# The final norm of the last token tile: a half in two pieces, two engines for the scaling, two queues for the store

## The chip, the cores and the metric

The kernel runs on one core of a Trainium2 chip. The metric is the device time of one execution in microseconds; before the change it was 1151.39 us, the median of three runs (1151.34 to 1152.82). About 0.2% (2.3 us) is what a measurement of this kernel can tell from no change.

## The reference, cut to what matters

Two transformer layers over 512 tokens of width 1024, each a token mixer and a dense MLP, then one last RMSNorm. The change touches the last projection of the second MLP and that norm:

```python
def rms_norm(x, g):
    xf = x.astype(jnp.float32)
    y = xf * lax.rsqrt(jnp.mean(xf * xf, axis=-1, keepdims=True) + EPS)
    return (y * g.astype(jnp.float32)).astype(x.dtype)

def squared_relu_mlp(h, w_up, w_down):
    a = jax.nn.relu(h @ w_up)
    return (a * a) @ w_down

        x = x + squared_relu_mlp(h, mlp_w_up[i], mlp_w_down[i])
    return rms_norm(x, final_norm)
```

## The kernel before, in words

The 512 tokens are four tiles of 128 rows (`NT` = 4); the residual `xt[t]` of each stays in SBUF as 128x1024 fp32. Products are taken in split precision: each operand is held as a high and a low part, and `mm3` (lines 227 to 229) issues three matmuls for one product. The MLP runs over 8 blocks of 512 hidden columns. The down projections of the first seven blocks go through `down_quarters`; the last block goes through `down` (line 1232), which is what the change edits.

`down` walks the four token tiles, and in each tile the two halves of 512 output columns. One half is 4 x 3 matmuls of 512 columns into one PSUM bank (`ps`, taken from banks 6, 7, 2, 3 in turn), then an addition of that bank into `xt[t]` by VectorE (line 1244), then the call `after(t, c)`. In the second MLP `after` is `Final.follow`, and it calls `rms_half`.

`rms_half` (line 430) does the final norm of a tile. On each half ScalarE squares `x` into the output tile `fo` as a throwaway and leaves the sum of the squares in a column of `rs_s` (line 436; on the chip an ACTIVATE and a short read of the accumulator). After the second half VectorE adds the two sums and the epsilon (line 440, 128x1), GpSimd raises this to the power -0.5 (line 441, `rs_y`, 128x1), and VectorE writes `x * y * gain` in two pieces of 512 columns (line 444). Behind each piece SyncE issues a store of 256 KB (line 1266), which waits for that piece alone. `fo` has two buffers, so a tile's first square waits for the stores of the tile two before it.

A scheduler orders each engine's instructions when the kernel is built; each engine then runs its own list in order and waits on semaphores. Behind the last store SyncE waits for all stores to land, and a barrier of all engines ends the program.

Of the kernel before, what the change touches and what calls it, by code (L numbers as in the profile page):

```python
# [11 lines left out]
F32 = mybir.dt.float32  # L12
F32R = mybir.dt.float32r
I32 = mybir.dt.int32
AF = mybir.ActivationFunctionType
OP = mybir.AluOpType
PSUM = bass.MemoryType.PSUM

P = 128
D = 1024  # L20
S = 512
NT = S // P
KD = D // P
CHUNK = 64
EPS = 1e-6
# [179 lines left out]
def trunk(ctx: ExitStack, tc: tile.TileContext, x, positions, attn_norm, mlp_norm, a_w_in, a_w_out,  # L205
          b_w_in, b_q_norm, b_kv_norm, b_w_q_up, b_w_kv_up, b_w_out, mlp_w_up, mlp_w_down,
          final_norm, out):
    nc = tc.nc
# [9 lines left out]
    class Banks:  # L218
        def __init__(self, *ids):
            self.ids, self.n = ids, 0  # L220
# [5 lines left out]
    def mm3(ps, lh, ll, rh, rl, first, last):  # L226
        nc.tensor.matmul(ps, lh, rh, start=first, stop=False)  # L227
        nc.tensor.matmul(ps, lh, rl, start=False, stop=False)  # L228
        nc.tensor.matmul(ps, ll, rh, start=False, stop=last)  # L229
# [3 lines left out]
    neghalf = const.tile([P, 1], F32, name="neghalf")  # L233
# [56 lines left out]
    ht = ctx.enter_context(tc.tile_pool(name="ht", bufs=1, reuse_waits="tile"))  # L290
# [5 lines left out]
    def gain(pool, row, n, tag="gain"):  # L296
        g = pool.tile([P, n], F32, name="gain", tag=tag)
        nc.sync.dma_start(g, bass.AP(tensor=row.tensor, offset=row.offset, ap=[[0, P], [1, n]]))
        return g

    xt = [const.tile([P, D], F32, name=f"x{t}") for t in range(NT)]
# [123 lines left out]
            cs = slice(c, min(c + 512, n))  # L425
            nc.vector.scalar_tensor_tensor(dst[:, cs], src[:, cs], y, g[:, cs], op0=OP.mult, op1=OP.mult)

    half_sums = []

    def rms_half(dst, src, g, c, done=None):  # L430

        cs = slice(c * 512, (c + 1) * 512)
        if c == 0:
            half_sums.append(ht.tile([P, 2], F32, name="rs_s", tag="rs2", bufs=3))
        ss = half_sums[-1]
        nc.scalar.activation(dst[:, cs], src[:, cs], AF.Square, scale=D ** -0.5, accum_out=ss[:, c:c + 1])
        if c == 1:
            half_sums.pop()
            y = ht.tile([P, 1], F32, name="rs_y", tag="rs", bufs=8)
            nc.vector.tensor_scalar(y, ss[:, 0:1], ss[:, 1:2], EPS, op0=OP.add, op1=OP.add)  # L440
            nc.gpsimd.tensor_tensor(y, y, neghalf, op=OP.pow)
            for i in range(2):
                cs = slice(i * 512, (i + 1) * 512)
                nc.vector.scalar_tensor_tensor(dst[:, cs], src[:, cs], y, g[:, cs], op0=OP.mult, op1=OP.mult)
                if done is not None:
                    done(cs)

    def to_feature_major(src, nk, hi, lo, t, banks):

        for k0 in range(0, nk, 4):  # L450
            n = min(4, nk - k0)
            ps = banks("tps")
            for k in range(n):
                nc.tensor.transpose(ps[:, k * P:(k + 1) * P], src[:, (k0 + k) * P:(k0 + k + 1) * P], ident)  # L454
            pv = ps[:, :n * P].rearrange("p (k t) -> p k t", k=n)
            h = hi[:, k0:k0 + n, t * P:(t + 1) * P]
            l = lo[:, k0:k0 + n, t * P:(t + 1) * P]
            nc.scalar.copy(h, pv)  # L458
            nc.vector.tensor_sub(l, pv, h.bitcast(F32))

    class Norm:
# [30 lines left out]
            with tc.high_priority(60):  # L492
                to_feature_major(self.h.pop(t), KD, self.hi, self.lo, t, self.banks)

        def follow(self, t, c):

            if c == 0:
                return
            if self.lag == 2 and t >= 2:
                self.turn(t - 2)  # L500
            self.scale(t)
            if self.lag == 1 and t:
                self.turn(t - 1)
# [13 lines left out]
    def out_proj(oh, ol, banks, after=None, held=0):  # L517

        n = oh.shape[1]
        ws = W.take(n, held)  # L520
        for t in range(NT):
            for c in range(2):
                cs = slice(c * 512, (c + 1) * 512)
                ps = banks("wo_ps")
                for j in range(n):
                    wh, wl = ws[j]
                    mm3(ps, oh[:, j, t * P:(t + 1) * P], ol[:, j, t * P:(t + 1) * P], wh[:, 0, cs], wl[:, 0, cs],
                        j == 0, j == n - 1)
                    if j % 2 == 1 and j < n - 1:
                        yield  # L530
                nc.vector.tensor_add(xt[t][:, cs], ps, xt[t][:, cs])
                if after is not None:
                    after(t, c)
                yield


# [162 lines left out]
    def mixer_a():  # L699
        with ExitStack() as sa:  # L700
# [255 lines left out]
            for i in range(2):  # L956
                for _ in proj_tiles(Banks(*((0, 1, 6, 7), (2, 3, 4, 5))[i]), lambda t, ps: q_done(i, t, ps)):
# [4 lines left out]
                    if n > 32 and n % 4 == 0:  # L962
                        plan.step(-6 + (n - 36) // 4)
            run(selection)
            plan.filler(44, 0.7, lazy(lambda: out_proj(*O[0], Banks(7))))
            plan.filler(60, 0.4, lazy(lambda: out_proj(*O[1], Banks(7))))
            plan.run()
            nm = Norm(mlp_norm[0], lag=2)
            run(out_proj(*O[2], Banks(4, 5, 6, 7), nm.follow))
        return nm  # L970

# [175 lines left out]
    def mlp(i, nm, follower):  # L1147
        with ExitStack() as sm:
# [3 lines left out]
            up_b, dn_b = Banks(0, 1, 4, 5), Banks(6, 7, 2, 3)  # L1152
# [11 lines left out]
            def up(b):  # L1164
                u = mp.tile([P, 4, S], F32, name="u", tag="u", bufs=2)
                if b == 0:

                    ws = W.take(2) + W.take(2, 2)
                    pp = [up_b("up") for _ in range(4)]
                    for f in range(4):  # L1170
                        up_mm(pp[f], ws[f // 2 * 2:][:2], f % 2, 0, S // 2)
                        if f % 2:
                            nm.turn(NT - 2 + f // 2)
                    for f in range(4):
                        up_mm(pp[f], ws[f // 2 * 2:][:2], f % 2, S // 2, S)
                        square(pp[f], u, f)
                    return u
                for c in range(FB // 256):
                    ws = W.take(2)
                    for f in range(2):  # L1180
                        ps = up_b("up")
                        up_mm(ps, ws, f, 0, S)
                        square(ps, u, 2 * c + f)
                return u

            def part(v):

                lh = mp.tile([P, 2, S // 2], F32R, name="lh", tag="lh", bufs=8)
                ll = mp.tile([P, 2, S // 2], F32R, name="ll", tag="ll", bufs=8)
                nc.scalar.copy(lh, v)  # L1190
                nc.vector.tensor_sub(ll, v, lh.bitcast(F32))  # L1191
                return lh, ll

            def blocks(u):

                return [[u[:, 2 * k:2 * k + 2, i * 256:(i + 1) * 256] for k in range(2)] for i in range(2)]
# [32 lines left out]
                        last = nc.vector.tensor_add(x[:, cs], pp[t], x[:, cs])  # L1229
                return last  # L1230

            def down(u, after):
                ops = [[part(v) for v in row] for row in blocks(u)]
                ws = W.take(FB // P)
                for t in range(NT):
                    ts = slice(t % 2 * P, (t % 2 + 1) * P)
                    for c in range(2):
                        cs = slice(c * 512, (c + 1) * 512)
                        ps = dn_b("dn")
                        for k in range(4):  # L1240
                            wh, wl = ws[k]
                            lh, ll = ops[t // 2][k // 2]
                            mm3(ps, lh[:, k % 2, ts], ll[:, k % 2, ts], wh[:, 0, cs], wl[:, 0, cs], k == 0, k == 3)
                        nc.vector.tensor_add(xt[t][:, cs], ps, xt[t][:, cs])
                        after(t, c)

            prev = up(0)
            last = None
            for b in range(1, NB):
                with tc.issue_after(last.ins) if last is not None else ExitStack():  # L1250
                    ops = left(prev)
                prev = up(b)
                last = down_quarters(ops)
            nxt = follower()
            down(prev, nxt.follow)
        return nxt

    class Final:
        def __init__(self):
            self.g = gain(ht, final_norm, D)  # L1260

        def follow(self, t, c):
            if c == 0:
                self.o = ht.tile([P, D], F32, name="fo", tag="h", bufs=2)
            o = self.o
            rms_half(o, xt[t], self.g, c, lambda cs: nc.sync.dma_start(out[0, t * P:(t + 1) * P, cs], o[:, cs]))

    nm = mixer_a()
    nm = mlp(0, nm, lambda: Norm(attn_norm[1]))
    nm = mixer_b(nm)  # L1270
    mlp(1, nm, Final)


# [22 lines left out]
```

## Time and profile before

| what | value |
|---|---|
| median of the runs | 1151.39 us (1151.34 to 1152.82) |
| the profiled execution's own time | 1150.95 us |
| its span | 1149.2 us |
| PE busy | 1117.5 us, 97% of the span |
| VectorE, ScalarE, GpSimd busy | 66%, 54%, 58% |
| granted TensorE clock, mean | 0.993 of full speed |

Engines are named PE (TensorE matmul), PEld (its weight loads), DVE (VectorE), ACT (ScalarE), POOL (GpSimd) and SP (SyncE); SPq is SyncE's issuing of DMAs. A timeline row gives the start in us from the span's start, the length in us, engine, line, operation, names (output<-input) and shapes; in brackets stands how long the engine was idle before it and what ended the wait. A span lies inside the execution's own time; 1.75 us lie around it.

### The profile page before, as it was taken

Reading aid. Unit: us, or ns where it says so; the run is one execution under the profiler, and the core shown is the slowest. Engines: PE = TensorE matmul, PEld = TensorE weight load, DVE = VectorE, ACT = ScalarE, POOL = GpSimd, SP = SyncE. Lnnn points to the kernel's source line nnn. Section 1 sums busy time; section 2 is a strip of 40 time slices with the busy share of each in tenths; the row PEclk is TensorE's granted clock in tenths of the full one; section 3 lists DMA queues with packets and bytes.
Section 4 is the critical chain, followed back from the end, with each engine's and each line's share of the span. In section 5 each row is a group of like instructions: output and inputs, shape, how many; then the busy total and the mean of one; then the engine's idle time right before and its main releaser. Section 6 shows DMA issues by size and latency. Waiting matters only on the chain.

```text
span 1149.2 us, 16018 instructions
## 1 busy us (share of the span) xinstructions
PE 1117.5 (97%) x5725; PEld 949.2 (83%) x5725; DVE 754.8 (66%) x1399; ACT 619.7 (54%) x1143; POOL 670.0 (58%) x508
## 2 busy tenths in 40 slices
PE   8999899989999999999999999899999999999997
PEld 7788788869888888888889898787988888888886
DVE  6699798673566466466566788676556466556664
ACT  6574896534544554454445776563564454464452
POOL 5498533543657857856702643554557756865772
PEclk9999999989999999999999999999999999999999
DMA  6413100242224314413322200111424313412402
GB/s 200 123 55 110 38 1 1 76 150 87 75 72 147 106 58 130 133 58 103 86 62 79 76 23 34 56 56 56 167 63 138 128 49 117 147 61 87 147 10 83
DMA packets 65465, 99.04 MB, mean 86 GB/s; under 512 B 3173, under 2 KB 41833, under 8 KB 65386
## 3 DMA queue, kind: packets, MB, share of 16 engines
q1 hardware_dynamic: 65386, 98.03, 26.9%
q8 instruction: 45, 0.74, 0.3%
q14 instruction: 34, 0.28, 0.1%
HBM read 95.92 MB, written 2.10 MB: 85 GB/s over the span
## 4 chain that ended last, share of the span: by engine, by line
PE 90%; DVE 3%; ACT 3%; issue 2%; POOL 1%; DMA 1%; SPq 0%; DVEq 0%; POOLq 0%; ACTq 0%
PE dn L1226 23%; PE up L227 10%; PE up L229 10%; PE up L228 10%; PE s_ps L560 3%; PE o_ps L622 3%; PE pt_ps L579 2%; PE wo_ps L227 2%; PE wo_ps L228 2%; PE wo_ps L229 2%; PE pp L227 2%; PE pp L229 2%; PE pp L228 2%; PE tps L454 1%; PE dn L228 1%
## 5 line engine op out<-in xcount | busy, mean ns | idle before, releaser
L148 POOL TENSOR_TENSOR w_lo<-quad,w_hi 128x512 fp32r<-128x512 f32 x196 | 274.7, 1433 | 163.1 <-ACT w_hi L143 155.7
L150 POOL TENSOR_TENSOR w_lo<-w_raw,w_hi 128x1024 fp32r<-128x1024 f32 (+4 forms) x117 | 264.4, 2278 | 86.7 <-ACT w_hi L143 71.6
L1229 DVE TENSOR_TENSOR x<-dn,x 128x512 f32<-128x512 f32 x196 | 134.9, 690 | 139.5 <-PE dn L1226 139.4
L228 PE MATMUL up<-hT_lo,w_hi 128*128 128x512 f32 (+1 forms) x576 | 210.8, 367 | 0.0
L227 PE MATMUL up<-hT_hi,w_hi 128*128 128x512 f32 (+1 forms) x576 | 210.3, 368 | 0.0
L229 PE MATMUL up<-hT_hi,w_lo 128*128 128x512 f32 (+1 forms) x576 | 208.8, 367 | 0.0
L143 ACT CAST w_hi<-w_raw 128x1024 fp32r<-128x1024 f32 (+6 forms) x112 | 111.7, 1006 | 141.1 <-PE dn L1226 62.2
L143 ACT CAST w_hi<-quad 128x1024 fp32r<-128x1024 f32 x98 | 101.2, 1050 | 100.0 <-DVE quad L86 71.7
L1226 PE MATMUL dn<-w_hi,lh 128*128 128x512 f32 x392 | 152.5, 389 | 0.0
L1226 PE MATMUL dn<-w_lo,lh 128*128 128x512 f32 x392 | 152.5, 389 | 0.0
L1226 PE MATMUL dn<-w_hi,ll 128*128 128x512 f32 x392 | 152.5, 389 | 0.0
L1191 DVE TENSOR_TENSOR ll<-u,lh 128x512 fp32r<-128x512 f32 x106 | 99.2, 966 | 40.7 <-ACT lh L1190 40.7
L229 PEld LDWEIGHTS up<-hT_hi,w_lo 128*128 128x128 f32 x576 | 109.1, 190 | 17.6
L227 PEld LDWEIGHTS up<-hT_hi,w_hi 128*128 128x128 f32 x576 | 109.0, 190 | 17.6 <-ACT hT_hi L458 0.2
L228 PEld LDWEIGHTS up<-hT_lo,w_hi 128*128 128x128 f32 x576 | 109.1, 190 | 17.4
L86 DVE TENSOR_TENSOR quad<-quad 128x1024 f32<-128x1024 f32 x56 | 68.4, 1221 | 65.3 <-POOL w_lo L148 65.3
L1190 ACT CAST lh<-u 128x512 fp32r<-128x512 f32 x106 | 62.9, 620 | 75.0 <-DVE u L1203 66.6
L1226 PEld LDWEIGHTS dn<-w_hi,ll 128*128 128x128 f32 x392 | 73.6, 188 | 15.3
L1226 PEld LDWEIGHTS dn<-w_hi,lh 128*128 128x128 f32 x392 | 73.6, 188 | 15.3
L1226 PEld LDWEIGHTS dn<-w_lo,lh 128*128 128x128 f32 x392 | 73.6, 188 | 15.3
L573 ACT ACTIVATE p<-p,m 128x128 f32<-128x128 f32 (+3 forms) x128 | 72.0, 564 | 16.3 <-DVE m L568 15.5
L592 ACT CAST pt_hi<-pt_ps 128x128 fp32r<-128x128 f32 (+3 forms) x128 | 53.0, 423 | 27.8 <-PE pt_ps L579 25.3
(237 smaller groups left out, 2249.8 us busy)
## 6 DMA issues: line engine op xcount, KB each, us to landing
w_raw<-in_mlp_w_up_dram SPq DMA_DIRECT2D x64, 512.0 KB, 3.7
quad<-in_mlp_w_down_dram SPq DMA_DIRECT2D x56, 512.0 KB, 3.6
w_raw<-in_a_w_in_dram SPq DMA_DIRECT2D x12, 512.0 KB, 3.6
w_raw<-in_a_w_out_dram SPq DMA_DIRECT2D x8, 512.0 KB, 3.2
w_raw<-in_mlp_w_down_dram SPq DMA_DIRECT2D x8, 512.0 KB, 4.5
w_raw<-in_b_w_out_dram SPq DMA_DIRECT2D x8, 512.0 KB, 3.7
x<-in_x_dram SPq DMA_DIRECT2D x4, 512.0 KB, 7.5
w_raw<-in_b_w_kv_up_dram SPq DMA_DIRECT2D x4, 512.0 KB, 3.9
```

The source lines that it names most:

```text
L86: self.nc.vector.tensor_sub(q[o], q[l], q[r])
L143: nc.scalar.copy(h, v)
L148: nc.gpsimd.tensor_sub(l[:, cs], v[:, cs], h[:, cs].bitcast(F32))
L150: (nc.gpsimd if engs[1] == "p" else nc.vector).tensor_sub(l, v, h.bitcast(F32))
L227: nc.tensor.matmul(ps, lh, rh, start=first, stop=False)
L228: nc.tensor.matmul(ps, lh, rl, start=False, stop=False)
L229: nc.tensor.matmul(ps, ll, rh, start=False, stop=last)
L573: nc.scalar.activation(U["p"][:, :N], U["p"][:, :N], AF.Exp, bias=U["m"], scale=-1.0, accum_out=pair["sums"][:, c:c + 1])
L1190: nc.scalar.copy(lh, v)
L1191: nc.vector.tensor_sub(ll, v, lh.bitcast(F32))
L1226: nc.tensor.matmul(pp[t], l[:, k, ts], r[:, k, :], start=first and k == 0 and m == 0, stop=k == 1 and m == 2, skip_group_check=True)
L1229: last = nc.vector.tensor_add(x[:, cs], pp[t], x[:, cs])
```

## The change

`down` now asks its follower for the column ranges of each tile (`cuts`). They are the two halves as before, but in the last tile the second half is cut into columns 512 to 768 and 768 to 1024. `rms_half` is gone; `Final.follow` holds the norm itself:

- The sums of squares of all tiles go to one tile `rs_f`, four columns for each token tile. The last tile has three sums; VectorE adds the first two and the epsilon, and then the third by a second instruction.
- In the last tile GpSimd multiplies the first half of `x` by the gain into `fo` as soon as that half has been squared.
- In the last tile the first half is then scaled by ScalarE (a copy with the per-row factor `y` as scale, in place) and the second half by VectorE as before. ScalarE issues the store of the half that it scaled, SyncE that of the other.
- Tiles 0 to 2 do what they did.

```diff
-                    for c in range(2):
-                        cs = slice(c * 512, (c + 1) * 512)
-                        ps = dn_b("dn")
+                    for c0, c1 in cuts(t):
+                        cs = slice(c0, c1)
+                        ps = dn_b("dn")[:, 0:c1 - c0]
...
-                        after(t, c)
+                        after(t, c0, c1)
...
+        def cuts(self, t):
+            return ((0, 512), (512, D)) if t < NT - 1 else ((0, 512), (512, 768), (768, D))
+
+        def follow(self, t, c0, c1):
+            if c0 == 0:
+                self.o, self.n = ht.tile([P, D], F32, name="fo", tag="h", bufs=2), 0
+            o, ss, n = self.o, self.s[:, t], self.n
+            self.n += 1
+            nc.scalar.activation(o[:, c0:c1], xt[t][:, c0:c1], AF.Square, scale=D ** -0.5, accum_out=ss[:, n:n + 1])
+            if n:
+
+                nc.vector.tensor_scalar(ss[:, 3:4], ss[:, n:n + 1], ss[:, 0:1] if n == 1 else ss[:, 3:4],
+                                        EPS if n == 1 else None, op0=OP.add, **({"op1": OP.add} if n == 1 else {}))
+            if t == NT - 1 and c0 == 0:
+                nc.gpsimd.tensor_mul(o[:, 0:512], xt[t][:, 0:512], self.g[:, 0:512])
+            if c1 < D:
+                return
+            y = ht.tile([P, 1], F32, name="rs_y", tag="rs", bufs=8)
+            nc.gpsimd.tensor_tensor(y, ss[:, 3:4], neghalf, op=OP.pow)
+            for i in range(2):
+                cs = slice(i * 512, (i + 1) * 512)
+                q = nc.sync
+                if t == NT - 1 and i == 0:
+                    nc.scalar.activation(o[:, cs], o[:, cs], AF.Copy, scale=y)
+                    q = nc.scalar
+                else:
+                    nc.vector.scalar_tensor_tensor(o[:, cs], xt[t][:, cs], y, self.g[:, cs], op0=OP.mult, op1=OP.mult)
+                q.dma_start(out[0, t * P:(t + 1) * P, cs], o[:, cs])
```

The order of instructions is the same on every engine up to the last token tile; only what follows differs. `x3_87` is the residual of the last tile, `x2_86` that of the tile before it, `dn` the PSUM bank, `fo` the output tile, `rs_s`, `rs_f` and `rs_y` the sums and the factor, and `gain` the gain. On VectorE, at the program's end, the order was:

```order
L1244 TENSOR_TENSOR x2_86<-dn_10740,x2_86 128x512
L440 TENSOR_SCALAR rs_y_10755<-rs_s_10738 128x1
L444 SCALAR_TENSOR_TENSOR fo_10737<-x2_86,rs_y_10755,gain_10627 128x512 x2
L1244 TENSOR_TENSOR x3_87<-dn_10762,x3_87 128x512
L1244 TENSOR_TENSOR x3_87<-dn_10779,x3_87 128x512
L440 TENSOR_SCALAR rs_y_10794<-rs_s_10777 128x1
L444 SCALAR_TENSOR_TENSOR fo_10776<-x3_87,rs_y_10794,gain_10627 128x512 x2
```

At the same place of VectorE it now is:

```order
L1227 TENSOR_TENSOR x2_86<-dn_10738,x2_86 128x512
L1259 TENSOR_SCALAR rs_f_10629<-rs_f_10629 128x1
L1274 SCALAR_TENSOR_TENSOR fo_10736<-x2_86,rs_y_10754,gain_10627 128x512 x2
L1227 TENSOR_TENSOR x3_87<-dn_10760,x3_87 128x512
L1227 TENSOR_TENSOR x3_87<-dn_10777,x3_87 128x256
L1227 TENSOR_TENSOR x3_87<-dn_10793,x3_87 128x256
L1259 TENSOR_SCALAR rs_f_10629<-rs_f_10629 128x1 x2
L1274 SCALAR_TENSOR_TENSOR fo_10774<-x3_87,rs_y_10809,gain_10627 128x512
```

The last addition is two of half the width, both small sums stand behind them, and one of the last two scalings is gone. On ScalarE the end, from the last conversions of weights on, was:

```order
L143 CAST w220_hi_10591<-w220_raw_10537 128x1024
L143 CAST w221_hi_10609<-w221_raw_10557 128x1024
L436 ACTIVATE fo_10659,rs_s_10660<-x0_84 128x512 x2
L436 ACTIVATE fo_10698,rs_s_10699<-x1_85 128x512 x2
L436 ACTIVATE fo_10737,rs_s_10738<-x2_86 128x512 x2
L436 ACTIVATE fo_10776,rs_s_10777<-x3_87 128x512 x2
```

At the same place of ScalarE it now is:

```order
L143 CAST w221_hi_10609<-w221_raw_10557 128x1024
L1256 ACTIVATE fo_10660,rs_f_10629<-x0_84 128x512 x2
L1256 ACTIVATE fo_10698,rs_f_10629<-x1_85 128x512 x2
L1256 ACTIVATE fo_10736,rs_f_10629<-x2_86 128x512 x2
L1256 ACTIVATE fo_10774,rs_f_10629<-x3_87 128x512
L1256 ACTIVATE fo_10774,rs_f_10629<-x3_87 128x256 x2
L1271 ACTIVATE fo_10774<-fo_10774,rs_y_10809 128x512
L1275 DMA out_0_dram<-fo_10774 128x512
```

The last square is two of half the width, and the scaling of the first half and its store have come behind them. GpSimd's list ended, from the last low parts of weights on, with:

```order
L150 TENSOR_TENSOR w221_lo_10610<-w221_raw_10557,w221_hi_10609 128x1024
L441 TENSOR_TENSOR rs_y_10677<-rs_y_10677,neghalf_69 128x1
L441 TENSOR_TENSOR rs_y_10716<-rs_y_10716,neghalf_69 128x1
L441 TENSOR_TENSOR rs_y_10755<-rs_y_10755,neghalf_69 128x1
L441 TENSOR_TENSOR rs_y_10794<-rs_y_10794,neghalf_69 128x1
```

At the same place of GpSimd it now is:

```order
L150 TENSOR_TENSOR w221_lo_10610<-w221_raw_10557,w221_hi_10609 128x1024
L1266 TENSOR_TENSOR rs_y_10678<-rs_f_10629,neghalf_69 128x1
L1266 TENSOR_TENSOR rs_y_10716<-rs_f_10629,neghalf_69 128x1
L1266 TENSOR_TENSOR rs_y_10754<-rs_f_10629,neghalf_69 128x1
L1262 TENSOR_TENSOR fo_10774<-x3_87,gain_10627 128x512
L1266 TENSOR_TENSOR rs_y_10809<-rs_f_10629,neghalf_69 128x1
```

The multiplication by the gain stands between the third and the last power. On PE the last 12 matmuls of 512 columns are 24 of 256, and SyncE issues seven of the eight stores.

## Rows read from the trace of the kernel before

**Rows 1.** The page: span, then busy time and share of each engine.

```profile
span 1149.2 us, 16018 instructions
...
PE 1117.5 (97%) x5725; PEld 949.2 (83%) x5725; DVE 754.8 (66%) x1399; ACT 619.7 (54%) x1143; POOL 670.0 (58%) x508
```

**Rows 2.** The page: shares of the chain that ended last, by engine.

```profile
PE 90%; DVE 3%; ACT 3%; issue 2%; POOL 1%; DMA 1%; SPq 0%; DVEq 0%; POOLq 0%; ACTq 0%
```

**Rows 3.** Timeline of PE, first and last matmul of the last half.

```profile
1139.63 0.39 PE L227 MATMUL dn<-w_hi,lh 128*128 128x512 f32 x1
...
1142.12 0.39 PE L229 MATMUL dn<-w_hi,ll 128*128 128x512 f32 x1
```

**Rows 4.** Timeline of DVE behind it.

```profile
1140.80 0.68 DVE L1244 TENSOR_TENSOR x<-dn,x 128x512 f32<-128x512 f32 x1
1142.55 0.69 DVE L1244 TENSOR_TENSOR x<-dn,x 128x512 f32<-128x512 f32 x1 [1.06 <-PE dn L229]
1144.03 0.21 DVE L440 TENSOR_SCALAR rs_y<-rs_s 128x1 f32<-128x1 f32 x1 [0.79 <-ACT fo L436]
1144.90 0.75 DVE L444 SCALAR_TENSOR_TENSOR fo<-x,rs_y,gain 128x512 f32<-128x512 f32 x1 [0.66 <-POOL rs_y L441]
```

**Rows 5.** Timeline of ACT in the last tile.

```profile
1141.57 0.63 ACT L436 ACTIVATE fo<-x 128x512 f32<-128x512 f32 x1 [3.01 <-DVE x L1244]
1142.10 0.19 ACT L436 ACTIVATION_READ_ACCUMULATOR fo<-x 128x1 f32 x1
1143.27 0.63 ACT L436 ACTIVATE fo<-x 128x512 f32<-128x512 f32 x1 [0.98 <-DVE x L1244]
1143.81 0.19 ACT L436 ACTIVATION_READ_ACCUMULATOR fo<-x 128x1 f32 x1
```

**Rows 6.** Timeline of POOL in the last tile.

```profile
1144.32 0.55 POOL L441 TENSOR_TENSOR rs_y<-rs_y,neghalf 128x1 f32<-128x1 f32 x1 [4.89 <-DVE rs_y L440]
```

**Rows 7.** Timeline of SyncE's issues, the last two stores.

```profile
1145.68 0.33 SPq L1266 DMA_DIRECT2D out_dram<-fo  x1
...
1146.35 0.33 SPq L1266 DMA_DIRECT2D out_dram<-fo  x1
```

**Rows 8.** DMA issues: times issued, KB each, median us to landing.

```profile
out_dram<-fo SPq DMA_DIRECT2D x8, 256.0 KB, 2.0
...
x<-in_x_dram SPq DMA_DIRECT2D x4, 512.0 KB, 7.5
```

**Rows 9.** Stretches: length, busy engines, PEclk, DMA share, GB/s.

```profile
1146.50:1147.00 0.50, 0.00 (x0) 0.00 (x0) 0.00 (x0) 0.00 (x0) 0.00 (x0) 1.00 0.96 377
1147.00:1147.50 0.50, 0.00 (x0) 0.00 (x0) 0.00 (x0) 0.00 (x0) 0.00 (x0) 1.00 0.97 373
1147.50:1148.00 0.50, 0.00 (x0) 0.00 (x0) 0.00 (x0) 0.00 (x0) 0.00 (x0) 0.68 0.78 299
```

**Rows 10.** Timeline of PE in the second MLP's start: 256 columns.

```profile
821.24 0.28 PE L229 MATMUL up<-hT_hi,w_lo 128*128 128x256 f32 x1
821.36 0.28 PE L227 MATMUL up<-hT_hi,w_hi 128*128 128x256 f32 x1
```

**Rows 11.** Groups by shape, weight loads: busy us, mean ns.

```profile
L229 PEld LDWEIGHTS dn<-w_hi,ll 128*128 128x128 f32 x64 | 12.0, 188 | 2.5
```

**Rows 12.** Groups by shape, DVE: out of PSUM, 256 columns.

```profile
L998 DVE TENSOR_TENSOR vv<-vp,vv 128x256 fp32r<-128x256 f32 x16 | 6.6, 413 | 1.9 <-ACT vv L997 1.8
```

**Rows 13.** Groups by shape, ACT: a square of 256; a per-row operand.

```profile
L420 ACT ACTIVATE sq<-nat 128x256 f32<-128x256 f32 x4 | 1.6, 410 | 0.0
...
L829 ACT ACTIVATE bias<-bias,lead 128x512 f32<-128x512 f32 x1 | 0.7, 724 | 4.8 <-DVE bias L826 4.8
```

**Rows 14.** Groups by shape, POOL: two full operands of 512 and 1024 columns.

```profile
L148 POOL TENSOR_TENSOR w_lo<-quad,w_hi 128x512 fp32r<-128x512 f32 x196 | 274.7, 1433 | 163.1 <-ACT w_hi L143 155.7 <-PE dn L1226 7.4
L150 POOL TENSOR_TENSOR w_lo<-w_raw,w_hi 128x1024 fp32r<-128x1024 f32 x100 | 239.1, 2410 | 76.1 <-ACT w_hi L143 62.6 <-PE up L228 12.1 <-DMA w_raw<-in_mlp_w_up_dram 1.0
```

**Rows 15.** Line 1229, DVE: ns min/median/max, first and last start.

```profile
L1229 DVE TENSOR_TENSOR x<-dn,x x196: 669/691/693, 303.1 to 1120.5; 128x512 f32<-128x512 f32 x196
```

More of the change, by code (lines that the diff above doesn't have):

```diff
@@ L426, in rms @@
             nc.vector.scalar_tensor_tensor(dst[:, cs], src[:, cs], y, g[:, cs], op0=OP.mult, op1=OP.mult)
-    half_sums = []
-    def rms_half(dst, src, g, c, done=None):
-        cs = slice(c * 512, (c + 1) * 512)
[L433 to L446, printed above, removed]
     def to_feature_major(src, nk, hi, lo, t, banks):
@@ L493, in turn @@
                 to_feature_major(self.h.pop(t), KD, self.hi, self.lo, t, self.banks)
-        def follow(self, t, c):
-            if c == 0:
+        def cuts(self, t):
+            return (0, 512), (512, D)
+        def follow(self, t, c0, c1):
+            if c1 < D:
                 return
@@ L532, in out_proj @@
                 if after is not None:
-                    after(t, c)
+                    after(t, c * 512, c * 512 + 512)
                 yield
@@ L1230, in down_quarters, with down @@
                 return last
-            def down(u, after):
+            def down(u, after, cuts):
                 ops = [[part(v) for v in row] for row in blocks(u)]
@@ L1236, in down @@
                     ts = slice(t % 2 * P, (t % 2 + 1) * P)
-                    for c in range(2):
-                        cs = slice(c * 512, (c + 1) * 512)
-                        ps = dn_b("dn")
+                    for c0, c1 in cuts(t):
+                        cs = slice(c0, c1)
+                        ps = dn_b("dn")[:, 0:c1 - c0]
                         for k in range(4):
@@ L1244, in down @@
                         nc.vector.tensor_add(xt[t][:, cs], ps, xt[t][:, cs])
-                        after(t, c)
+                        after(t, c0, c1)
             prev = up(0)
@@ L1254, in mlp @@
             nxt = follower()
-            down(prev, nxt.follow)
+            down(prev, nxt.follow, nxt.cuts)
         return nxt
@@ L1260, in __init__, with cuts, follow @@
             self.g = gain(ht, final_norm, D)
[L1262 to L1266, printed above, removed]
+            self.s = ht.tile([P, NT, 4], F32, name="rs_f", tag="rs2", bufs=1)
+        def cuts(self, t):
+            return ((0, 512), (512, D)) if t < NT - 1 else ((0, 512), (512, 768), (768, D))
+        def follow(self, t, c0, c1):
+            if c0 == 0:
[8 more added lines that the diff above has]
+                nc.gpsimd.tensor_mul(o[:, 0:512], xt[t][:, 0:512], self.g[:, 0:512])
+            if c1 < D:
+                return
[10 more added lines that the diff above has]
+                q.dma_start(out[0, t * P:(t + 1) * P, cs], o[:, cs])
     nm = mixer_a()
```

## The prediction

> **What bounds the kernel now.** Read the page's busy times first. PE is busy for 97% of the span of 1149.2 us [rows 1], and the chain of work that ended last runs through PE for 90% of it [rows 2]. So nearly all of the time is matmul time, and no edit of the norm can touch it. What is left for this change is the stretch behind the last matmul, and there the timelines of the engines have to be laid side by side.
>
> The last half of the last tile starts on PE at 1139.63 and its twelfth matmul at 1142.12, 0.226 us apart on average; the last ends at 1142.12 + 0.39 = 1142.51 [rows 3]. Then each step waits for the one before it: the addition at 1142.55 for 0.69 us [rows 4], the square at 1143.27, whose sum has been read at 1143.81 + 0.19 = 1144.00 [rows 5], the small sum at 1144.03 for 0.21 us [rows 4], the power from 1144.32 to 1144.87 [rows 6], the first scaling at 1144.90 for 0.75 us [rows 4]. The stores are issued at 1145.68 and 1146.35 [rows 7], and a store lands 2.0 us after its issue [rows 8], so the last at 1148.35. The remaining 0.85 us to 1149.2 are waits and the closing barrier. The whole tail behind PE is 6.7 us, 0.6% of the span; 2.3 us, what a measurement can tell from no change, is a third of it.
>
> **The change, part by part.** All engines keep their order up to the last tile, so everything up to 1139.63 is priced at nothing.
>
> *Matmuls of 256 columns.* Twelve become 24. The trace has such matmuls in the MLP's first block: they start 0.12 us apart and take 0.28 us each [rows 10]. The 24th then starts 23 x 0.12 = 2.76 us after 1139.63, at 1142.39, and ends at 1142.67: 0.16 later than now. Bounds: half of 0.226 would be 0.113 and an end at 1142.51, no later than now. A weight load takes 0.188 us [rows 11], and if the loads set the pace, the 24th would start 4.3 us later and end near 1144.24, 1.7 later. I take 0.12, since the rows of exactly this shape, each with its own load, show it: the loads overlap.
>
> *The addition and the square of 256.* An addition out of PSUM over 256 columns has a row of 0.413 us [rows 12] against 0.69: 0.28 saved. A square of 256 takes 0.410 us [rows 13] against 0.63 [rows 5]: 0.22 saved; the read of the sum stays at 0.19. The first piece costs nothing: its matmuls end at 1139.63 + 11 x 0.12 + 0.28 = 1141.23, its addition follows the one of 1140.80 and ends at about 1141.9, and its square follows that of 1141.57 [rows 4, 5] and ends at about 1142.7, while PE is still at the second piece. If PE gave no such cover, these 0.41 + 0.41 + 0.19 us would stand on the path.
>
> *The second small sum.* It waits for the last square, as the only one did, and takes the same 0.21 us. The first waits for the first piece's square and stands on VectorE behind the last addition, so it runs at about 1143.1, beside the last square; its 0.21 us are hidden. Behind it wait only the second sum and the last scaling, which need later things anyway.
>
> *GpSimd's multiplication.* It waits for the first square's sum, read at 1142.10 + 0.19 = 1142.29 [rows 5]. The nearest row, two full operands of 512 columns, takes 1.433 us [rows 14], so it ends at about 1143.76. Queued behind it on GpSimd is the power, which everything waits for. The power is ready at 1142.71 (addition) + 0.41 + 0.03 + 0.32 + 0.19 (square and read) + 0.03 + 0.21 (sum) + 0.08 = 1143.98, so the multiplication hides, with 0.2 us to spare. Above: at the 2.41 us of 1024 columns [rows 14] the power would be 0.76 later; below it can give nothing. I take 1.433. Does it slow the addition beside it? Over 196 additions of this kind, with GpSimd busy 58% of the span [rows 1], the shortest is 669 ns and the longest 693 [rows 15]: no.
>
> So the power runs from 1143.98 to 1144.53 instead of 1144.32 to 1144.87: 0.34 earlier (0.16 later from PE, 0.28 + 0.22 earlier from the two halved steps).
>
> *Scaling on two engines.* VectorE's piece takes 0.75 us. ScalarE's copy with a factor by row has no row of its own; the nearest, an ACTIVATE of 512 columns out of SBUF with an operand by row, takes 0.724 us [rows 13]; without one the square takes 0.63. Either end is hidden beside VectorE's 0.75. Both pieces are ready at about 1145.3, and the second, which now follows 0.67 us behind the first [rows 7], no longer waits for its turn.
>
> *Stores on two queues.* Here the trace speaks against a gain. The two last stores, all from one queue, keep the DMA engines 0.96 and 0.97 busy at 377 and 373 GB/s [rows 9]; 262 KB at 375 GB/s are 0.70 us, and the second store is issued 0.67 us behind the first. So the engines are full from the first byte of the one to the last of the other. Issued together they still need one after the other's time: the last lands 2.0 + 0.7 us after the common issue, 1145.34 + 2.7 = 1148.04, against 1148.35. The 0.67 us gained by scaling side by side are lost again in the queue, and 0.3 of the 0.34 us remain. The Trainium skill (DMA: Bandwidth & Descriptors, Issuing engines are not separate DMA queues) says the same as a rule: DMAs issued by several engines run on the same 16 DMA engines, and issuing them at once saves only the sequencer's issue time. By that rule the third edit could save at most one issue of 0.33 us; by the rows not even this, since SyncE had ended its first issue at 1146.01 and sat until 1146.35 waiting for VectorE.
>
> What no row shows is a store issued by ScalarE. Below: its bytes could flow beside the other's at full pace, and the last would land at 1145.34 + 2.0, 0.7 earlier still. Above: the longest time to landing in the rows is 7.5 us, of the first loads [rows 8]. I take SyncE's 0.33 and 2.0, the row of the same transfer.
>
> **The sum.** 0.3 us less, made against the profiled execution's 1150.95 us: 1150.65. That execution lies 0.4 below the median of the runs, 1151.39; carried over to the median, the forecast is 1151.1 us, 0.03% less. What I expect to see measured is no change.
>
> **The rivals.**
>
> - *The queues run side by side.* For it: the second store's landing took 2.0 us although the first was still under way. Against it: the share of 0.97 leaves no room. It would give 1151.39 - 1.0 = 1150.4 us, still no change.
> - *The weight loads set the pace.* For it: a load of 0.188 us is longer than 0.12. Against it: the pitch in rows 10. With the 1.7 instead of 0.16 the sum is +1.2: 1152.6 us, slower, but within 0.2%.
> - *GpSimd is late.* At 2.41 us for the multiplication the power slips by 0.76: 1151.1 + 0.76 = 1151.9 us.
> - *The other side: ScalarE's store lands late.* It is the first of its queue, and the program ends only when it has landed. For it: the first loads of SyncE's queue took 7.5 us. Against it: those were 512 KB each, several under way at once. At 7.5 us it lands at 1145.34 + 7.5 = 1152.8, 4.5 after the present last landing: 1155.9 us. It decides for slower from a landing time of 1148.35 + 2.3 - 1145.34 = 5.3 us on.
> - *Faster by over 0.2%* would need 2.3 of the 6.7 us behind PE. Even both favourable ends together (side by side 1.0, PE's 0.16 saved) give 1.2 us. It is left for what a build may move unseen, such as where tiles lie in memory.
>
> **How the numbers follow.** The forecast 0.78, side by side 0.06, weight loads 0.04, GpSimd late 0.04, ScalarE's store late 0.04, unseen gain 0.04. The first four lie within 0.2%: same 0.92; faster 0.04; slower 0.04. The terms alone would hold the time between 1150.4 and 1152.6; the runs of before spread from 1151.34 to 1152.82 and the profiled one lies 0.44 under their median, so I widen this to 1149.8 to 1153.0.
>
> **What would show each step.** In the profile after: the last 24 matmuls 0.12 us apart; the last addition about 0.41 us long; the multiplication over before the power becomes ready; the power ending 4.90 us behind the start of the last half on PE (1139.63) instead of 5.24; the two issues at the same time; and the DMA engines full for 1.4 us without a gap, the last landing 2.7 us behind the issues. The forecast is wrong if the 256-column matmuls stand 0.19 apart, if the power waits for GpSimd's own multiplication, if both stores land 2.0 us after issue, or if the span differs before 1139.63, where nothing was moved.

## The result: slower by half a per cent

The changed kernel takes 1157.82 us, the median of five runs (1155.75 to 1161.32); the kernel before took 1152.82 beside it (1151.34 to 1153.17). The ratio is 1.0054, with a 95% interval from 1.0040 to 1.0069. The prediction had 1151.1 us and no change, with slower at 0.04. The profiled execution of the changed kernel took 1160.22 us, 2.4 above its median.

### The profile after

The page of the changed kernel, span and busy times [rows 1] and the chain's shares [rows 2]:

```profile
span 1158.4 us, 16046 instructions
...
PE 1127.5 (97%) x5737; PEld 952.0 (82%) x5737; DVE 748.2 (65%) x1400; ACT 621.1 (54%) x1146; POOL 671.7 (58%) x509
...
PE 89%; DVE 4%; ACT 3%; issue 2%; POOL 1%; DMA 1%; SPq 0%; POOLq 0%; ACTq 0%; DVEq 0%
```

The span is 9.2 us longer and PE is busy 10.0 us longer, with only 12 more matmuls, all short. ScalarE and GpSimd gained less than 2 us each, and VectorE is busy 6.6 us less. So the loss is matmul time, not waiting.

First the tail, since the forecast was made of it. These are timelines of the changed kernel, from the last half's first matmul to the last issue, as [rows 3 to 7] are for the kernel before:

```profile
1149.14 0.28 PE L227 MATMUL dn<-w_hi,lh 128*128 128x256 f32 x1
...
1151.83 0.28 PE L229 MATMUL dn<-w_hi,ll 128*128 128x256 f32 x1
```

```profile
1151.75 1.27 POOL L1262 TENSOR_TENSOR fo<-x,gain 128x512 f32<-128x512 f32 x1 [2.88 <-ACT fo L1256]
1151.88 0.18 ACT L1256 ACTIVATION_READ_ACCUMULATOR fo<-x 128x1 f32 x1
1152.14 0.42 DVE L1227 TENSOR_TENSOR x<-dn,x 128x256 f32<-128x256 f32 x1 [0.89 <-PE dn L229]
1152.48 0.20 DVE L1259 TENSOR_SCALAR rs_f<-rs_f 128x1 f32<-128x1 f32 x1
1152.60 0.42 ACT L1256 ACTIVATE fo<-x 128x256 f32<-128x256 f32 x1 [0.53 <-DVE x L1227]
1152.92 0.19 ACT L1256 ACTIVATION_READ_ACCUMULATOR fo<-x 128x1 f32 x1
1153.14 0.21 DVE L1259 TENSOR_SCALAR rs_f<-rs_f 128x1 f32<-128x1 f32 x1 [0.46 <-ACT fo L1256]
1153.43 0.55 POOL L1266 TENSOR_TENSOR rs_y<-rs_f,neghalf 128x1 f32<-128x1 f32 x1 [0.42 <-DVE rs_f L1259]
1154.01 0.72 ACT L1271 ACTIVATE fo<-fo,rs_y 128x512 f32<-128x512 f32 x1 [0.91 <-POOL rs_y L1266]
1154.02 0.75 DVE L1274 SCALAR_TENSOR_TENSOR fo<-x,rs_y,gain 128x512 f32<-128x512 f32 x1 [0.66 <-POOL rs_y L1266]
1154.77 0.41 ACTq L1275 DMA_DIRECT2D out_dram<-fo  x1
```

```profile
1154.83 0.33 SPq L1275 DMA_DIRECT2D out_dram<-fo  x1
```

Stretches behind the issues (columns as in [rows 9]):

```profile
1155.50:1156.00 0.50, 0.00 (x0) 0.00 (x0) 0.00 (x0) 0.00 (x0) 0.00 (x0) 1.00 0.69 270
1156.00:1156.50 0.50, 0.00 (x0) 0.00 (x0) 0.00 (x0) 0.00 (x0) 0.00 (x0) 0.60 1.04 406
1156.50:1157.00 0.50, 0.00 (x0) 0.00 (x0) 0.00 (x0) 0.00 (x0) 0.00 (x0) 0.50 0.97 369
1157.00:1157.50 0.50, 0.00 (x0) 0.00 (x0) 0.00 (x0) 0.00 (x0) 0.00 (x0) 0.50 0.02 4
```

DMA issues of the stores (count, KB each, median us from issue to landing; [rows 8]):

```profile
out_dram<-fo SPq DMA_DIRECT2D x7, 256.0 KB, 2.0
out_dram<-fo ACTq DMA_DIRECT2D x1, 256.0 KB, 2.8
```

Count from the last half's start, 1139.63 before and 1149.14 after. The 24 matmuls stand (1151.83 - 1149.14) / 23 = 0.117 us apart. The power ends 1153.43 + 0.55 - 1149.14 = 4.84 behind (5.24 before), the stores are issued at 5.63 and 5.69 (6.06 and 6.72), the last landing in the trace's DMA records is at 8.39 (8.71), the end of the span at 9.29 (9.55). The tail became 0.3 us shorter, as forecast.

So the whole loss lies ahead of the last half, which starts 1149.14 - 1139.63 = 9.5 us later, in a part in which no engine's order was changed. The groups of PE by shape (line, operation, count, busy us, mean ns) name it. Before:

```profile
L227 PE MATMUL up<-hT_hi,w_hi 128*128 128x512 f32 x448 | 174.3, 389 | 0.0
...
L1226 PE MATMUL dn<-w_hi,lh 128*128 128x512 f32 x392 | 152.5, 389 | 0.0
```

After:

```profile
L227 PE MATMUL up<-hT_hi,w_hi 128*128 128x512 f32 x448 | 174.4, 389 | 0.0
...
L1209 PE MATMUL dn<-w_hi,lh 128*128 128x512 f32 x392 | 154.9, 395 | 0.0
```

The up projection is as before; each matmul of the down projection takes 6 ns longer. What counts for a full PE is the distance of the starts. At the same time of the second MLP, in the last block's down projection before:

```profile
1127.61 0.39 PE L229 MATMUL dn<-w_hi,ll 128*128 128x512 f32 x1
...
1128.97 0.39 PE L229 MATMUL dn<-w_hi,ll 128*128 128x512 f32 x1
```

and after, still in the block ahead of it, with matmuls of the same shape. From the first to the last shown it is six steps in both:

```profile
1127.67 0.39 PE L1209 MATMUL dn<-w_lo,lh 128*128 128x512 f32 x1
...
1129.07 0.39 PE L1209 MATMUL dn<-w_lo,lh 128*128 128x512 f32 x1
```

That is 1.36 / 6 = 0.227 us before and 1.40 / 6 = 0.233 after. With 1356 matmuls of this shape in both MLPs, 6 ns each make 8.1 us. Less the 0.3 of the tail that is 0.7% of the time; the interval measured is 0.40 to 0.69%. The remaining 1.4 of the 9.5 us fit the clock: near 125 us the granted clock stood at 0.50, the lower of TensorE's two levels (1.2 GHz), from 123.7 to 127.1 before and from 121.9 to 128.7 after, in both behind 12 to 14 us in which PE was idle for about a fifth to a quarter; its other falls are as long in both. These 3.4 us more at half the rate are worth up to 1.7 us. Executions of one kernel differ by up to 6 us among themselves, so nothing finer can be read from the times.

Why should these matmuls differ? The diff changes one thing that reaches beyond the last tile: the tag `rs2`. Its three buffers of two sums, 32 bytes each, became one buffer of 64 bytes. So it takes 32 bytes less, and all tiles allocated behind it lie 32 bytes lower in each partition. Start addresses in bytes, in the two built programs (bracketed: the remainder by 256):

```
tile                   before        after
w_hi (first buffer)     50176 [0]     50176 [0]
hT_hi                  103424 [0]    103424 [0]
tail (unused filler)   136544        136512
u                      136704 [0]    136672 [224]
lh (first buffer)      153088 [0]    153056 [224]
ll (first buffer)      169472 [0]    169440 [224]
oh (first mixer)       194208 [160]  194176 [128]
```

`lh` and `ll` are the stationary operands of `dn`, those that a weight load puts into TensorE; the weights `w_hi` and `w_lo` are the moving ones, which stream past them. This was the theory to test: `lh` and `ll` lie on multiples of 256 bytes before and off them after, and that costs 6 ns per matmul. The rival: something in the new code of the norm, not the places, disturbs the MLP.

### The profile page after: what moved, and what is told of

It reads as the page before. It is cut to its first block, busy times and chain, and to the rows that moved or that the text cites. A ratio compares the mean times of both kernels' runs of the same rounds, so it can differ in the third digit from the quotient of the medians.

```text
span 1158.4 us, 16046 instructions
## 1 busy us (share of the span) xinstructions
PE 1127.5 (97%) x5737; PEld 952.0 (82%) x5737; DVE 748.2 (65%) x1400; ACT 621.1 (54%) x1146; POOL 671.7 (58%) x509
## 4 chain that ended last, share of the span: by engine, by line
PE 89%; DVE 4%; ACT 3%; issue 2%; POOL 1%; DMA 1%; SPq 0%; POOLq 0%; ACTq 0%; DVEq 0%
PE dn L1209 24%; PE up L227 10%; PE up L229 10%; PE up L228 10%; PE s_ps L543 3%; PE o_ps L605 3%; PE pt_ps L562 2%; PE wo_ps L227 2%; PE wo_ps L229 2%; PE wo_ps L228 2%; PE pp L227 2%; PE pp L229 2%; PE pp L228 2%; PE tps L434 1%; PE dn L227 1%
## 5 line engine op out<-in xcount | busy, mean ns | idle before, releaser
L1209 PE MATMUL dn<-w_lo,lh 128*128 128x512 f32 x392 | 154.9, 395 | 0.0
L1209 PE MATMUL dn<-w_hi,lh 128*128 128x512 f32 x392 | 154.9, 395 | 0.0
L1174 DVE TENSOR_TENSOR ll<-u,lh 128x512 fp32r<-128x512 f32 x106 | 88.3, 863 | 38.4 <-ACT lh L1173 38.4
```

Source lines behind the costliest of these rows:

```text
L1209: nc.tensor.matmul(pp[t], l[:, k, ts], r[:, k, :], start=first and k == 0 and m == 0, stop=k == 1 and m == 2, skip_group_check=True)
```

## The experiments

All are edits of the kernel before or of the changed one. "dn" is the distance of the starts of the 512-column `dn` matmuls, the median over the trace; where two numbers stand, those of the three groups differ. The filler is the tile `tail` of the table above, which only takes up room. Runs of before beside them had medians of 1151.6 to 1153.1 us.

### Places against code

**a_pad**: the changed kernel, with the 32 bytes given back by the filler tile.

```diff
-    tail = pad.tile([P, 40], F32, name="tail")
+    tail = pad.tile([P, 48], F32, name="tail")
```

> The changed kernel with the padding tile `tail` 48 columns wide instead of 40. The sums' tile of the changed kernel takes 64 bytes in each partition where the three tiles before took 96, so all tiles allocated behind it (among them `lh` and `ll`, the stationary operands of the down projections) lie 32 bytes lower; the wider padding puts them back where they were. Placement theory: the matmuls of `dn` start 0.227 us apart again instead of 0.2335, the span is 1149.2 - 0.3 = 1148.9 us and the time 0.9997 of before, within 0.998 to 1.0015. Tail theory (the edits of the last tile cost the time, ScalarE's store above all): still 1.004 to 1.007. Third theory (the gain or loss is the build's own and not the placement's): anything, with `dn` at 0.2335.

Measured: 1153.3 us, ratio 1.0004 [0.9993, 1.0015], dn 227 ns. The loss is gone and all of the changed code is still there. The few tenths that the tail gains are too small to be seen in these times.

**b_shift**: the kernel before, with the filler at 32 columns and nothing else, so the places of the changed kernel with the old code.

> The kernel before with `tail` 32 columns wide instead of 40, and no other edit: all tiles behind it lie 32 bytes lower, as in the changed kernel, and the last norm is the old one. Placement theory: `dn` 0.2335 us apart, 1368 matmuls x 6.5 ns = 8.9 us more in the span where all are hit, 1.004 to 1.008 of before. Tail theory: 1.000, `dn` at 0.227.

Measured: 1160.46 us, ratio 1.0066 [1.0051, 1.0081], dn 234 ns. The loss is there without any of the changed code:

```profile
L1226 PE MATMUL dn<-w_hi,lh 128*128 128x512 f32 x392 | 154.8, 395 | 0.0
```

The two settle the question: it is the places, and the rival falls.

### Which tile, and which step of bytes

**b_lh** and **b_ll**: the kernel before; only `lh`, or only `ll`, lies off multiples of 256 (a tile 16 columns longer, used from its column 8, so that its buffers start at remainders of 32, 96, 160 and 224). The edit of b_lh:

```diff
-                lh = mp.tile([P, 2, S // 2], F32R, name="lh", tag="lh", bufs=8)
+                lh = mp.tile([P, S + 16], F32R, name="lh", tag="lh", bufs=8)[:, 8:8 + S].rearrange("p (a b) -> p a b", a=2)
```

> The kernel before with only the high parts `lh` moved: each buffer is 64 bytes longer and its content starts 32 bytes in; `ll` and the rest stay on multiples of 64 bytes. `lh` is the stationary operand of two of the three matmuls of a product. If a weight load from a start off 64 bytes is what costs time, and each load its own share: 912 of the 1368 matmuls slow, 5.9 us, 1.0035 to 1.006, and the matmuls with `ll` keep 0.227. If it is the distance between the two operands' addresses or another tile behind the padding (`u`, `quad`), this moves little: 0.999 to 1.0015.

> The kernel before with only the low parts `ll` moved by 32 bytes in the same way. Each load its own share: 456 matmuls slow, 3.0 us, 1.0015 to 1.0035, the matmuls with `lh` keep 0.227. If one load off its boundary holds up its two neighbours as well: as much as with `lh`, or as the whole shift. If the operands' start does not matter: 0.999 to 1.0015.

Measured: `lh` alone 1.0048 [1.0031, 1.0066], dn 231 to 232 ns; `ll` alone 1.0059 [1.0046, 1.0073], dn 231 to 235. Either alone brings most of the loss, and the matmuls with the other operand are slower too. That each load off its place costs its own share is wrong: `ll` is one load in three. Since the buffers have four different remainders here, b_ll32 below gives all of them the same.

**b_p64**, **b_p128**, **b_p256**: the kernel before, with the filler at 56, 72 and 104 columns, so everything behind lies 64, 128 or 256 bytes higher.

> The kernel before with `tail` 56 columns wide: everything behind it lies 64 bytes higher, `lh` and `ll` on multiples of 64 bytes but not of 128. If a start on 64 bytes is all that a stationary operand needs: `dn` 0.227 us apart, 0.9985 to 1.0015 of before. If it must lie on 128 or more: pitch 0.231 to 0.235, 1.004 to 1.007. What speaks for the second: in the changed kernel `oh` lies on a multiple of 64, not of 512, and the output projection still stands at 0.232.

> The same with 128 bytes (`lh`, `ll` on multiples of 128, not of 256). Boundary 64 or 128: pitch of `dn` 0.227, span 1148 to 1152. Boundary 256 or 512: 0.231 to 0.235, span 1154 to 1159.

> The same with 256 bytes (`lh`, `ll` on multiples of 256, not of 512). Boundary 64 to 256: pitch of `dn` 0.227, span 1148 to 1152. Boundary 512: 0.231 to 0.235.

Measured: +64 bytes 1.0079 [1.0053, 1.0105], dn 233; +128 one run of 1159.39 us, dn 232; +256 one run of 1152.27 us, dn 227. Of the steps tried only the 256 is harmless. Groups by shape, +128 and then +256:

```profile
L1226 PE MATMUL dn<-w_hi,lh 128*128 128x512 f32 x392 | 154.7, 395 | 0.0
```

```profile
L1226 PE MATMUL dn<-w_hi,lh 128*128 128x512 f32 x392 | 152.6, 389 | 0.3 <-ACT w_hi L143 0.3
```

**b_rest**: everything behind the filler 32 bytes lower, as in b_shift, but `lh` and `ll` back on multiples of 256 (tiles 64 columns longer, used from column 8).

> Before with the pad tile at 32 columns, so that u, quad and the mixers' tiles lie 32 bytes lower as in the slower kernels, while lh and ll are taken from longer tiles (a view from column 8 of 64 columns more) and start on multiples of 256 bytes again. If the stationary operands alone decide: dn at 227 ns and 0.999 to 1.001 of before. If u, quad, or whatever else moved has a share: above 1.003, or dn above 229.

Measured: 1151.38 us, ratio 0.9996 [0.9984, 1.0008], dn 227. `u` and the rest of the shifted tiles cost nothing measurable; the matmul's operands alone make the loss. Since these tiles are longer as well, this is also the control for the longer tiles of b_lh and b_ll.

**b_hT**: the kernel before, with `hT_hi` and `hT_lo` 32 bytes higher (the second moves because the first's tile is longer) and the filler shortened by as much, a line that is left out here.

```diff
-            self.hi = ht.tile([P, KD, S], F32R, name="hT_hi", tag="hT_hi")
+            self.hi = ht.tile([P, KD * S + 8], F32R, name="hT_hi", tag="hT_hi")[:, 8:8 + KD * S].rearrange("p (a b) -> p a b", a=KD)
```

> Before with hT_hi and hT_lo 32 bytes higher, off multiples of 256, and everything behind them in its old place. hT_hi is the moving operand of up (1728 matmuls) and the stationary one of pp (288 matmuls of 512 columns). If only a stationary operand's start matters: up stays at 227 ns, pp goes from 227 to 231-235, and the time is 1 to 2 us above before. If any operand's start matters: up at 231-235 too, and 9 to 12 us above before.

Measured: one run of 1162.51 us, 9.4 above before. The up projection, in which `hT` is the moving operand, goes from 227 to 234 ns, and `pp`, in which it is the stationary one, from 227 to between 232 and 234; dn stays at 227. Of the two cases expected the second came out: the moving operand's start counts as well.

```profile
1099.76 0.39 PE L227 MATMUL up<-hT_hi,w_hi 128*128 128x512 f32 x1
...
1101.16 0.39 PE L227 MATMUL up<-hT_hi,w_hi 128*128 128x512 f32 x1
```

Six steps in 1.40 us, as in the slow `dn` above.

Matmuls of 256 columns go the other way. In b_hT the 16 steps between these two matmuls of the up projection's first block take 1.87 us, 0.117 each, against 0.12 before [rows 10]:

```profile
828.04 0.28 PE L227 MATMUL up<-hT_hi,w_hi 128*128 128x256 f32 x1
...
829.91 0.28 PE L228 MATMUL up<-hT_lo,w_hi 128*128 128x256 f32 x1
```

The last 24 matmuls of `dn` agree: 0.117 us apart in the changed kernel, off their places, and (1147.41 - 1144.66) / 23 = 0.120 in a_pad, on them:

```profile
1144.66 0.28 PE L227 MATMUL dn<-w_hi,lh 128*128 128x256 f32 x1
...
1147.41 0.28 PE L229 MATMUL dn<-w_hi,ll 128*128 128x256 f32 x1
```

So the loss of 6 ns is one of the 512-column matmuls; those of 256 columns gain 3. Why is open.

**b_ll32**: the kernel before, with every buffer of `ll` exactly 32 bytes off a multiple of 256, and every buffer of `lh` on one.

> Before with every buffer of ll exactly 32 bytes off a multiple of 256 and every buffer of lh on one (in the earlier run of ll alone the buffers lay at eight different offsets). If one misaligned load in three lengthens the pitch of its neighbours too: all three dn groups at 231-235 and 1157-1160. If each load lengthens only one matmul: one group at 231-235, two at 227, and about 1155.

Measured: one run of 1162.73 us, at a mean granted clock of 0.989 where the run beside it had 0.993, so the groups say more than the time. By shape:

```profile
L1226 PE MATMUL dn<-w_lo,lh 128*128 128x512 f32 x392 | 156.7, 400 | 0.0
L1226 PE MATMUL dn<-w_hi,lh 128*128 128x512 f32 x392 | 154.7, 395 | 0.0
L1226 PE MATMUL dn<-w_hi,ll 128*128 128x512 f32 x392 | 152.5, 389 | 0.0
```

The order is `w_hi,lh`, `w_lo,lh`, `w_hi,ll`. The matmul just ahead of `ll`'s is 11 ns longer than the 389 of before, the one ahead of that 6, and `ll`'s own not at all. Neither expectation had this. Together it is 17 ns for three, against 3 x 6 = 18 with all three loads off: one load off its place costs as much as three. The distances from each start to the next agree, 233, 239 and 228 ns in this order where 227 stood before. Why is open.

### The tail, edit by edit

Three kernels for the tail, all with the filler at 48 columns, as in a_pad. **a_sp**: a_pad with both last stores issued by SyncE.

```diff
                     nc.scalar.activation(o[:, cs], o[:, cs], AF.Copy, scale=y)
-                    q = nc.scalar
```

> The changed kernel with the padding of 48 columns (old places) and one more edit: both stores of the last tile are issued by SyncE. The time is read from the start of the last half on PE (its first matmul of 256) to the last landing: 8.46 us with two queues, 8.71 in the kernel before. If the DMA engines are full anyway, one queue costs at most the second issue's 0.33 us, less what two queues lose by interleaving: 8.4 to 8.7. If the second queue is what shortened the tail: 8.9 or more.

**a_2half**: a_sp without the second cut (`cuts` returns the two halves for every tile).

> The changed kernel with the old places, both last stores on SyncE and the last half as one piece of 512 columns. The prediction's sum: no eighth of an us for the second piece's loads, but add 692 ns for 413 and square 720 for 410 behind the last matmul; from the last half's first matmul to the last landing 0.2 to 0.45 us more than the 8.31 of the version in two pieces. If the first piece's add and square hid nothing: within 0.1 of it.

**a_dve**: a_sp without GpSimd's multiplication and ScalarE's scaling; VectorE scales both halves.

> The changed kernel with the old places and both last stores on SyncE, without GpSimd's multiplication ahead and without ScalarE's scaling: VectorE scales the two halves one after the other. If the two scalings side by side earn what VectorE's second one costs: the second store is issued 0.6 to 0.75 us later than the 6.11 of the version with them, and the last landing is 0.2 to 0.7 later. If the stores' transfers hide it (the two share the DMA engines): within 0.15 of 8.31.

All in us from the start of the last half on PE (landings by the trace's DMA records; single executions):

| kernel | power ends | stores issued | last landing | end |
|---|---|---|---|---|
| before | 5.24 | 6.06, 6.72 | 8.71 | 9.55 |
| a_2half | 5.24 | 6.02, 6.45 | 8.65 | 9.49 |
| a_dve | 4.91 | 5.72, 6.42 | 8.42 | 9.26 |
| a_sp | 4.91 | 5.69, 6.11 | 8.31 | 9.15 |
| a_pad | 4.91 | 5.69, 5.76 | 8.46 | 9.37 |
| after | 4.84 | 5.63, 5.69 | 8.39 | 9.29 |

The cut is worth 8.65 - 8.31 = 0.34. The two scalings side by side bring the second issue 0.31 forward (6.42 to 6.11) and the landing only 0.11: in a_sp SyncE waits for itself, its two issues taking 0.81 us together (first row; below it a_dve, where the second waits for VectorE).

```profile
1148.10 0.81 SPq L1274 DMA_DIRECT2D out_dram<-fo  x2
```

```profile
1146.53 0.33 SPq L1270 DMA_DIRECT2D out_dram<-fo  x1
...
1147.23 0.33 SPq L1270 DMA_DIRECT2D out_dram<-fo  x1
```

The expectation for a_dve of 0.6 to 0.75 in the issue was wrong for that reason; that the transfers hide it was right. The second queue brings its store's issue 0.35 forward (6.11 to 5.76) and the last landing 0.15 back (8.31 to 8.46). The expectation for a_sp had one queue no better than 8.4 in either of its cases, so both missed this. That two queues land later is read from one execution each.

### A version with the operands in place

**best**: a_sp, with the mixers' `oh` and `ol`, stationary operands of `wo_ps` that lie off multiples of 256 in both kernels (in the first mixer at the remainders of the table, in the second partly at others), moved onto them by more buffers of a small tile allocated ahead.

```diff
-                    U["m"] = pool.tile([P, 1], F32, name="m", tag="m", bufs=4)
+                    U["m"] = pool.tile([P, 1], F32, name="m", tag="m", bufs=7 if wide else 5)
```

> The changed kernel with the pad tile at 48 columns (old places), both last stores on SyncE, and the mixers' tiles oh and ol (stationary operands of the matmuls into wo_ps) moved to multiples of 256 bytes by three and one more 32-byte buffers of m. Theory (a stationary operand off a multiple of 256 bytes lengthens its matmul's pitch): wo_ps from 231-235 ns to 227, 384 matmuls at about 6 ns, so 2.3 us less, and the tail's 0.4 us less: 0.997 to 0.999 of before. Rival (it is a matter of the MLP tiles alone): wo_ps stays at 231-235 and the time at 0.9995 to 1.000.

Measured: 1151.16 us against 1152.4, ratio 0.9987 [0.9975, 1.0000]. By the ratios to before it beats the changed kernel clearly, and the kernel before at the edge of what can be told. The groups of `wo_ps`, before and then best:

```profile
L228 PE MATMUL wo_ps<-w_lo,oh 128*128 128x512 f32 x128 | 50.7, 396 | 0.0
L229 PE MATMUL wo_ps<-w_hi,ol 128*128 128x512 f32 x128 | 49.2, 398 | 0.0
```

```profile
L228 PE MATMUL wo_ps<-w_lo,oh 128*128 128x512 f32 x128 | 50.2, 392 | 0.0
L229 PE MATMUL wo_ps<-w_hi,ol 128*128 128x512 f32 x128 | 48.8, 394 | 0.0
```

4 ns of each are gone, not 6: the median distances of the starts fall from between 232 and 235 ns to between 227 and 232, and part of the matmuls stay slow with all four operands on multiples of 256. What else holds these is open.

## Why the prediction was wrong, step by step

- **PE's share.** Right as a reading, and wrong in what it was used for: "no edit of the norm can touch it" held for the norm's instructions and not for its tiles.
- **"All engines keep their order up to the last tile, so everything up to 1139.63 is priced at nothing."** This is the step that failed. The order was kept and 9.5 us came up all the same, about 8 of them in `dn`, since the time of a matmul also hangs on where its operands lie; the diff showed a tile's size and buffer count change, and that was read as order alone. a_pad and b_shift show it from both sides.
- **The rivals.** Where tiles lie was named, but with 0.04 and as a gain. Read afterwards, the trace of before held a hint, no proof: `up`, `dn` and `pp` all stood at a median of 227 ns with operands on multiples of 256, `wo_ps` at 232 to 235 with `oh` off them. By that a shift of `dn`'s operands had more to lose than to gain. The other side of the forecast was put on ScalarE's store landing late; it landed 2.8 us after its issue, not 7.5.
- **Matmuls of 256 columns.** Right: 0.117 us apart against 0.12, and 0.120 in a_pad, where the operands lie as before; the loads did not set the pace.
- **Addition, square and power.** Right: 0.42 us each against 0.41, and the power ends 0.40 earlier in the tail (0.33 in a_pad) against 0.34.
- **GpSimd's multiplication.** 1.27 us against 1.43. It ends at 1151.75 + 1.27 = 1153.02, ahead of the power's start at 1153.43. The spare time was 0.4 us instead of 0.2.
- **Scaling on two engines and two queues.** Right as a sum: the DMA engines are full from the first byte on, the last landing 2.7 us behind the common issue, as forecast, and 0.32 earlier than before against 0.31. By a_pad's 8.46 it is 0.25: part of the 0.32 came from the moved operands, by which the 256-column matmuls gain 3 ns each, and that was luck. The Trainium skill (DMA: Bandwidth & Descriptors, Issuing engines are not separate DMA queues) has several issuers on the same 16 DMA engines, saving only issue time. The traces agree and go further: the issue saved was 0.35 us, and none of it reached the landing.

The forecast for the tail was met within 0.1 us. The time was missed, 1157.82 us against 1151.1, because of the 8 us (by the trace) that the tail's small tile cost the MLPs.

## What to carry to other kernels

A change of a tile's size or number of buffers moves every tile allocated behind it, and can alter the time of code that was not touched; so compare the start addresses of the two builds, not only the order of instructions. Before trusting a forecast of some tenths of a microsecond, see whether operands of the matmuls that fill TensorE keep their place, and keep both stationary and moving ones of 512-column matmuls on multiples of 256 bytes, or give the shift back with a filler. The places do not explain all: `wo_ps` stayed partly slow on them, and matmuls of 256 columns were a little faster off them. When a trace is longer in a part where nothing was moved, compare the distance of the starts of the commonest instruction first.

## What of the hardware was not expected

- In `dn`, `up` and `pp` a 512-column matmul of fp32 data starts 227 ns (median) after the one before it when stationary and moving operands start on multiples of 256 bytes, and 231 to 235 ns after it when one lies off (`dn` at 32, 64 and 128 bytes, `up` and `pp` at 32; 228 to 239 in b_ll32). Matmuls of 256 columns in `dn` and `up` go from 120 to 117 ns instead. The time of `dn`'s weight load stays at the 188 ns of [rows 11]; in the changed kernel:

```profile
L1209 PEld LDWEIGHTS dn<-w_hi,ll 128*128 128x128 f32 x392 | 73.5, 188 | 18.0
```

- One misaligned stationary operand in three lengthens the two matmuls that run ahead of its own, by 11 and 6 ns (b_ll32). The Trainium skill (TensorE: Matmul & The Clock Gate, Step-by-step: what each phase is for) gives TensorE two read ports, so that loading the next weights takes nothing from the running matmul. That agrees with 227 ns with a load of 188 beside it when all lies in place. In b_ll32 the running matmul pays all the same when the next weights lie off their place; whether it pays in read bandwidth no run here shows.
- The issue of a last store took ScalarE 0.41 us (one execution's row), and SyncE 0.33.
